# Uncharged preparation work in a one-core encoder layer: k, v blocks and sums of w_out taken out of the convolution's pacing, gate products and last w_out loads moved by a slot or more

## The chip, the core and the metric

The kernel runs on one core of one Trainium2 chip. The core has a matrix engine (TensorE, PE in the profile; the load of its weights is the line PEld) and three others: VectorE (DVE), ScalarE (ACT) and GpSimd (POOL). A fifth engine, SyncE (SP), issues the transfers (DMA). Each engine works off its own instructions in order; between engines, semaphores make an instruction wait for another. The metric is the device time of the one core in microseconds, the median of several runs.

## The reference

One layer of an encoder runs over 18 blocks of 128 tokens (two of a prompt, sixteen of a sample) with 16 learned meta tokens in front. Cut to what matters:

```python
h = rmsnorm(z, norm_w)
proj = einsum('bld,de->ble', h, w_in)                # 1024 -> 2816 columns
q, k, v, g_att, c_val, c_glu, g_conv = split(proj)
q = rmsnorm(q by head, q_norm_w); k = rmsnorm(k by head, k_norm_w)
att = windowed_gqa(q, k, v, sink) * silu(g_att)      # 8 heads, 2 of k and v, window 128, ALiBi, sink
u = c_val * sigmoid(c_glu)                           # 512 channels
y = depthwise convolution of u, width 31, + conv_b
cnv = silu(layernorm(y)) * silu(g_conv)              # norm over the 512 channels
out = z + concat(att, cnv) @ w_out                   # 1024 -> 1024
```

All is float32. A product is made of three passes on PE with operands that are split in a high and a low part.

## The kernel before

**Two chunks, eleven units.** The tokens are cut into six groups of 384 columns (the first 400), three to a chunk. For each chunk PE goes through eleven units of w_in, 256 columns each: four for the convolution's value and gate (U_C), two for the convolution's gate g_conv, two for g_att, one for k and v (U_KV), two for q (U_Q). A projection writes a PSUM tile pj; lines L1014 and L1030 are its matmuls (L1030 has the tokens on the partitions and serves k, v and q, one block of 128 tokens at a time). The last two units, called ws_6 and ws_7 in the program, run in the second chunk beside the layer norm and the first attention blocks.

**The convolution and its pacing.** DVE does the depthwise convolution, 31 taps for each of four channel tiles and each chunk (L1097). The taps wait in a queue in the code, and a small accountant hands them out while the program is written: tick(ns) gives credit for PE time that has passed, every tap takes 1.04 * 1167 + 135 = 1349 from it, and owe(ns) takes credit for other DVE work. So owe has no instruction of its own: it only makes the taps, and what follows them, come later in the program.

**The layer norm.** When a chunk's tap queue has been empty for LN_WAIT ticks (9 in the first chunk, 1 in the second), tick hands out one layer norm block of 128 tokens per call, ten blocks in the second chunk. A block is three steps: four transposes of y into PSUM (lnt, L250) with statistics on DVE (mv) and an inverse root on POOL; the normalisation on DVE into zn (L263, three buffers); four transposes back (lnu, L269), Silu on ACT into the same zn (L272) and a store to cd (L275). The attention later loads it as cn (L445).

**The attention and the output.** After the layer norm come 160 attention slots, eight to a block of 128 queries. A slot holds scores (S, L466), the maximum and exponentials (sb, L524 and L536, with a factor es taken in on POOL, L562), transposes of the probabilities (pT_c, pT_m, pT_x), their copies (ptiles, L588, L598, and on POOL with a mask, L590), the values (O, L616), and a piece of the output product. spread(b), called behind each of the 18 blocks of the two last q units, writes the first 14 slots between them from the eighth block on; attention_rest writes the others. Output products (yb, L721) go by pairs of blocks, 16 slots to a pair, in the order of the table JOBS; the table acts says in which slot of a pair the gate g_conv and the norm are loaded (load_mix: tiles gc and cn), multiplied on POOL (mix_conv, L695), subtracted (mix_diff), split into high and low parts (two_parts, cast on ACT L679, rest on DVE L680), and so on. The first product of a pair is c1, in slot 15.

**w_out.** Instead of four products of 2 by 2 blocks the kernel takes sums and differences of w_out's parts (c1, s1 to s4, t0, t1). presplit_sums makes these 14 operands (seven for each of two halves), in the second chunk beside the convolution, and stores them; pieces come back by load_apart and load_wo. Twelve are loaded from spread (WO_AT); load_wo 12 to 17 and the last load_apart follow in attention_rest. later(k, f) runs f k ticks later; the six loads use the buffers of the projections' operands.

**Who sets the order.** A scheduler places the instructions of each engine by its own estimate of their times. Once the attention's buffers are open, POOL keeps the order of the code instead; in attention_rest PE does too. All transfers go through SP's queue, which holds eight at a time: each waits for the one eight before it.

Of the kernel before, what the change touches and what calls it, by code (L numbers as in the profile page):

```python
# [82 lines left out]
PIECES_W = [("c1", 0), ("c1", 1), ("s3", 0), ("s3", 1), ("s2", 0), ("s2", 1), (6, 0), (6, 1), (7, 0), (7, 1)]  # L83
# [45 lines left out]
def hymba_kernel(  # L129
# [58 lines left out]
    def owe(ns):  # L188
        credit[0] -= ns

    def later(k, f):
        due.setdefault(clock[0] + k, []).append(f)
# [188 lines left out]
    def presplit_sums(i):  # L381

        raw = {}
        for key, e, nh in ((11, 4 + i, 0), (21, i, 0), (12, 4 + i, 1), (22, i, 1)):
            raw[key] = sp.tile([P, 2, 400], F32, tag="xt", name=f"wor{key}_{i}", bufs=XTB)[:, :, :UW]
            src = w_out[e][:, 512 * nh : 512 * nh + 512].rearrange("p (a n) -> p a n", n=UW)
            nc.sync.dma_start(raw[key], src)

        def operand(name, key):
            both = sp.tile([P, D], F32R, tag="xn", name=f"wo{name}_{i}")  # L390
            hi, lo = (both[:, 512 * k : 512 * k + 512].rearrange("p (a n) -> p a n", n=UW) for k in range(2))
            nc.scalar.copy(hi, raw[key])
            nc.vector.tensor_tensor(lo, raw[key], hi, op=ALU.subtract)
            owe(700)
            later(1, lambda: nc.sync.dma_start(wod[PIECES_W.index((name, i))], both.bitcast(F32)))

        def minus(dst, x, y):
            nc.vector.tensor_tensor(raw[dst], raw[x], raw[y], op=ALU.subtract)
            owe(700)

        steps = (
            ("c1", 11, None),
            ("t1", 21, (11, 12, 11)),
            ("s4", 22, (12, 22, 12)),
            ("s1", 11, (22, 22, 11)),
            ("s3", 12, (21, 21, 22)),
            ("s2", 22, None),
            ("t0", 21, None),
        )

        def step(name, key, diff):
            operand(name, key)
            if diff:
                minus(*diff)

        for k, args in enumerate(steps):
            later(2 + k, lambda args=args: step(*args))

    def load_apart(i):
        if i < 2:  # L420
            t = pool["b"].tile([P, D], F32R, tag=f"wa{i}", name=f"wa{i}", bufs=1)
        else:
            t = cst["pt" if i < APART else "rest"][:, 6:8].rearrange("p a n -> p (a n)")
        wo[PIECES_W[i]] = t
        nc.sync.dma_start(t.bitcast(F32), wod[i])

    def load_wo(idx):

        if idx % 3 == 0:
            slot = idx // 3  # L430
            wo_slot[slot] = xp.tile([P, ND, 400], F32R, tag=("xh", "xl")[slot % 2], name=f"wo{slot}")
        flat = wo_slot[idx // 3].rearrange("p a n -> p (a n)")
        i = APART + idx
        t = wo[PIECES_W[i]] = flat[:, D * (idx % 3) : D * (idx % 3) + D]
        nc.sync.dma_start(t.bitcast(F32), wod[i])
# [5 lines left out]
    def load_mix(b):  # L441
        gct[b] = pool["b"].tile([P, 4, P], F32, tag="gc", name=f"gc{b}", bufs=2)
        nc.sync.dma_start(gct[b], gd[4:8, :, P * b : P * b + P].rearrange("j p n -> p j n"))
        cnt[b] = pool["b"].tile([P, 4, P], F32, tag="cn", name=f"cn{b}", bufs=2)
        nc.sync.dma_start(cnt[b].rearrange("p j n -> p (j n)"), cd[b])  # L445
# [236 lines left out]
    def with_rest(f):  # L682
        pending.append(f)
        while "rest" in cst and pending:
            pending.pop(0)()
# [8 lines left out]
    def mix_conv(b):  # L694
        nc.gpsimd.tensor_tensor(cnt[b], cnt[b], gct[b], op=ALU.mult)  # L695

    def mix_diff(p):
        nc.gpsimd.tensor_tensor(temp(0), cnt[2 * p + 1][:, 0:NS, :], cnt[2 * p][:, 0:NS, :], op=ALU.subtract)
        diff[p] = True
# [53 lines left out]
    for p in range(NB // 2):  # L753
        b0, b1 = 2 * p, 2 * p + 1
        for rel, f in (
            (5, lambda b0=b0: load_mix(b0)),
            (7, lambda b1=b1: load_mix(b1)),
            (9, lambda p=p: load_x(p, (0, 1))),
            (10, lambda b0=b0: mix_conv(b0)),
            (11, lambda b1=b1: mix_conv(b1)),  # L760
            (12, lambda p=p: with_rest(lambda: mix_diff(p))),
            (12, lambda p=p: load_x(p, (1, 1))),
            (13, lambda b1=b1: with_rest(lambda: two_parts("c1", cnt[b1][:, 0:NS, :]))),
            (14, lambda: with_rest(lambda: two_parts("s3", temp(0)))),
            (17, lambda b0=b0: two_parts(("c", 0), cnt[b0][:, NS:4, :])),
            (17, lambda p=p: load_x(p, (0, 0))),
            (20, lambda b1=b1: two_parts(("c", 1), cnt[b1][:, NS:4, :])),
            (18, lambda p=p: load_x(p, (1, 0))),
            (18, lambda p=p: add_kept(p, (1, 1), 0)),
            (20, lambda p=p: add_kept(p, (0, 0), 1)),  # L770
            (21, lambda p=p: add_kept(p, (1, 0), 0)),
        ):
            acts.setdefault(16 * p + rel, []).append(f)
        for rel, name, es in JOBS:
            to = late_jobs if name == "s3" else jobs
            if p == LAST and name in ("t1", (1, 0)):
                for c0 in (0, 256):
                    to.setdefault(16 * p + rel, []).append((p, name, es, c0, 256))
            else:
                to.setdefault(16 * p + rel, []).append((p, name, es))  # L780
# [53 lines left out]
    def attention_rest():  # L834
        for _ in range(2):
            tick(0)
        cst["man"].close()
        att_pools.enter_context(tc.manual_schedule(engines=MAN2))
        rest = wl.tile([P, ND, 2, UW], F32R, tag="ws", name="rest")
        cst["rest"] = rest.rearrange("p a b n -> p (a b n)").rearrange("p (i n) -> p i n", n=512)  # L840
        for k in range(6):
            later(1 + k, lambda k=k: load_wo(12 + k))
        later(7, lambda: load_apart(len(PIECES_W) - 1))
        while slots:
            slot_step(*slots.pop(0))
        while work_left():
            tick(3000)
        att_pools.close()
        wr_pools.close()
        left_pools.close()  # L850

    if True:
# [321 lines left out]
        def kv_block(ws, g, o, rows, b):  # L1174
            ps = proj_te(ws, g, o, rows)
            rk = head_norm(ps, rows, KV, f"k{b}")
            vs = sp.tile([P, KV, 2, HD], F32R, tag="vs", name=f"vs{b}", bufs=3)
            pv = ps[:rows, P : 2 * P].rearrange("p (h e) -> p h e", e=HD)
            nc.scalar.copy(vs[:rows, :, 0, :], pv)
            nc.vector.tensor_tensor(vs[:rows, :, 1, :], pv, vs[:rows, :, 0, :], op=ALU.subtract)  # L1180
            vflat = vs[:rows].rearrange("p a b e -> p (a b e)").bitcast(F32)
            store(vmd if b < 0 else vd[b], vflat)
            kn = sp.tile([P, KV, HD], F32, tag="kn", name=f"kn{b}")
            owe(800)

            def fin():
                pk = ps[:rows, 0:P].rearrange("p (h e) -> p h e", e=HD)
                nc.vector.tensor_tensor(
                    kn[:rows],
                    pk,  # L1190
                    rk[:rows, :KV].unsqueeze(2).to_broadcast([rows, KV, HD]),
                    op=ALU.mult,
                )
                later(1, fin2)

            def fin2():
                pt = psum.tile([P, 512], F32, tag="d", name=f"kt{b}")
                nc.tensor.transpose(pt[:, :rows], kn[:rows].rearrange("p a e -> p (a e)"), ident[:rows, :rows])
                ks = sp.tile([P, 2 * P], F32R, tag="ks", name=f"ks{b}")
                nc.scalar.mul(ks[:, :rows], pt[:, :rows], kscale[:, 0:1])  # L1200
                nc.vector.scalar_tensor_tensor(
                    ks[:, rows : 2 * rows], pt[:, :rows], kscale[:, 0:1], ks[:, :rows], op0=ALU.mult, op1=ALU.subtract
                )
                to = (kmd if b < 0 else kd[b]).rearrange("(h p) k l n -> p h k (l n)", h=2)
                for kv in range(KV):
                    part = ks[HD * kv : HD * kv + HD, : 2 * rows].bitcast(F32)
                    store(to[:, :, kv, :], part.unsqueeze(1).to_broadcast([HD, 2, 2 * rows]))

            later(1, fin)
# [262 lines left out]
```

## Time and profile before

| | before |
|---|---|
| time, median of 3 runs | 955.06 us (953.53 to 955.95) |
| profiled execution | 954.25 us, span 952.4 |
| PE busy | 930.4 us, 98% |
| DVE busy | 774.5 us, 81% |
| ACT busy | 449.8 us, 47% |
| POOL busy | 364.1 us, 38% |
| HBM read, written | 115.83 MB, 65.85 MB |

The span goes from the first to the last instruction of the profiled execution; its time is 1.85 us longer. A row of the trace reads: start, duration, engine, line, operation, output <- inputs, shape, count, and in square brackets the idle time before it with what ended it. A row of a stretch reads: from:to, its length, PE's busy time and number of matmuls, the clock that PE was granted (1.00 is full), the mean busy share of the 16 DMA engines, and GB/s. A row of waits reads: who waited, for whom, us in total, times, longest. In the chain of waits each row is a start, a duration and what the end of the program waited for in that time.

### The profile page before, as it was taken

The numbers are of one execution on the slowest core, as the hardware profiler recorded it, in microseconds if no ns is written. First come the engines' busy times: TensorE is split into PE (matmuls) and PEld (weight loads), VectorE is DVE, ScalarE is ACT, GpSimd is POOL, SyncE is SP. The second block draws the span as 40 slices with busy tenths as digits, with TensorE's granted clock in tenths as the row PEclk, the third lists the DMA queues.
The fourth block names the chain that finished last, engine by engine and source line by source line (L and its number), as shares of the span: only waits on it lengthen the run. The fifth ranks groups of instructions, "written<-read, shape, count | busy, mean of one in ns | idle before, by whom it ended". The sixth has DMA issues, their size and how long they took to land.

```text
span 952.4 us, 16892 instructions
## 1 busy us (share of the span) xinstructions
PE 930.4 (98%) x5734; PEld 878.5 (92%) x5734; DVE 774.5 (81%) x1340; ACT 449.8 (47%) x1233; POOL 364.1 (38%) x553
## 2 busy tenths in 40 slices
PE   8999999999999999999999998799999999999998
PEld 8999999999999999999999988677888888888887
DVE  5579999997977779999997545579887887887874
ACT  7432112353458732011112248567676677676762
POOL 4310000273559300000001343587766466555654
PEclk9999999999999999999999999999999999999999
DMA  8584345675755686333334785996556665665421
GB/s 303 168 282 183 133 174 182 249 268 206 226 154 189 204 290 241 133 122 130 138 132 139 212 242 188 380 341 184 173 176 179 177 195 151 182 197 169 133 96 55
DMA packets 146342, 182.80 MB, mean 192 GB/s; under 512 B 40944, under 2 KB 106816, under 8 KB 146128
## 3 DMA queue, kind: packets, MB, share of 16 engines
q1 hardware_dynamic: 146256, 181.72, 58.3%
q8 instruction: 45, 0.74, 0.3%
q14 instruction: 41, 0.34, 0.1%
HBM read 115.83 MB, written 65.85 MB: 191 GB/s over the span
## 4 chain that ended last, share of the span: by engine, by line
PE 81%; DVE 6%; POOL 3%; DMA 3%; ACT 3%; issue 2%; SPq 0%; POOLq 0%; ACTq 0%; DVEq 0%
PE pj L1014 42%; PE yb L721 16%; PE pj L1030 11%; PE O L616 4%; PE S L466 3%; DVE rest L680 1%; PE pT_m L582 1%; PE pT_c L582 1%; DVE ptiles L599 1%; PE pT_x L582 1%; DVE sb L524 1%; DMA cd<-zn 1%; DMA qd<-qr 1%; ACT sb L536 1%; DMA kd<-ks 1%
## 5 line engine op out<-in xcount | busy, mean ns | idle before, releaser
L1014 PE MATMUL pj<-xh,ws 128*128 128x384 f32 (+1 forms) x1536 | 395.9, 338 | 0.1
L1097 DVE SCALAR_TENSOR_TENSOR y<-us,cw,y 128x1167 f32<-128x1167 f32 x240 | 329.2, 1430 | 0.1
L1014 PEld LDWEIGHTS pj<-xh,ws 128*128 128x128 f32 x1536 | 280.0, 188 | 0.4 <-ACT xh L1262 0.4
L1014 PE MATMUL pj<-xl,ws 128*128 128x384 f32 (+1 forms) x768 | 260.9, 340 | 0.1
L721 PE MATMUL yb<-wo,rest 128*128 128x512 f32 (+1 forms) x717 | 190.8, 399 | 0.0
L1030 PE MATMUL pj<-ws,xh 128*128 128x256 f32 (+1 forms) x880 | 165.9, 286 | 3.9 <-ACT sqq L1131 3.7
L721 PEld LDWEIGHTS yb<-wo,rest 128*128 128x128 f32 x717 | 125.9, 189 | 22.6 <-DVE rest L680 0.2
L1014 PEld LDWEIGHTS pj<-xl,ws 128*128 128x128 f32 x768 | 144.1, 188 | 0.5 <-DVE xl L952 0.4
L1030 PEld LDWEIGHTS pj<-ws,xh 128*128 128x128 f32 (+1 forms) x880 | 137.9, 189 | 4.9 <-ACT sqq L1131 3.9
L1030 PE MATMUL pj<-ws,xl 128*128 128x256 f32 (+1 forms) x440 | 125.1, 284 | 0.0
L1122 ACT ACTIVATE go<-pj 128x384 f32<-128x384 f32 x48 | 23.6, 491 | 151.4 <-PE pj L1014 142.8
L536 ACT ACTIVATE sb<-sb,nm 128x304 f32<-128x304 f32 (+5 forms) x144 | 77.9, 541 | 30.6 <-DVE nm L524 28.5
L177 POOL TENSOR_SCALAR ssk<-ssk 128x2 f32<-128x2 f32 x18 | 10.1, 561 | 211.3 <-ACT sqk L1136 209.3
L524 DVE CUSTOM_DVE_ANT_0 sb<-S,bias,vec 128x304 f32<-128x304 f32 (+5 forms) x144 | 73.8, 515 | 20.4 <-PE S L466 19.4
L562 POOL TENSOR_SCALAR sb<-sb,es 128x304 f32<-128x304 f32 (+5 forms) x144 | 78.3, 563 | 24.7 <-PE pT_x L582 9.9
L1030 PEld LDWEIGHTS pj<-ws,xl 128*128 128x128 f32 (+1 forms) x440 | 83.4, 190 | 0.2
L466 PE MATMUL S<-kw,q 128*128 128x304 f32 (+5 forms) x288 | 63.6, 303 | 2.4 <-ACT keptFalse L739 1.2
L466 PEld LDWEIGHTS S<-kw,q 128*128 128x128 f32 x288 | 52.4, 188 | 14.3 <-ACT keptFalse L739 2.3
L177 POOL TENSOR_SCALAR ssq<-ssq 128x4 f32<-128x4 f32 (+2 forms) x55 | 24.9, 453 | 97.7 <-ACT xn L877 72.5
L644 POOL TENSOR_TENSOR at<-at,ga 128x256 f32<-128x256 f32 x36 | 28.0, 777 | 85.7 <-DVE at L638 85.7
L732 DVE TENSOR_TENSOR yo<-yb,yo 128x512 f32<-128x512 f32 (+1 forms) x55 | 36.9, 671 | 14.9 <-PE yb L721 14.8
L990 DVE TENSOR_TENSOR ws<-wraw,ws 128x512 fp32r<-128x512 f32 x50 | 34.8, 726 | 8.2 <-ACT ws L989 8.2
(156 smaller groups left out, 1369.5 us busy)
## 6 DMA issues: line engine op xcount, KB each, us to landing
wd<-ws SPq DMA_DIRECT2D x36, 512.0 KB, 5.9
ws<-wd SPq DMA_DIRECT2D x36, 512.0 KB, 6.3
wraw<-in_w_in SPq DMA_DIRECT2D x52, 256.0 KB, 6.2
xn<-in_z SPq DMA_DIRECT2D x18, 512.0 KB, 5.4
gd<-go SPq DMA_DIRECT2D x48, 192.0 KB, 2.0
wo<-wod SPq DMA_DIRECT2D x18, 512.0 KB, 7.9
yo<-in_z SPq DMA_DIRECT2D x36, 256.0 KB, 3.3
out_y<-yo SPq DMA_DIRECT2D x35, 256.0 KB, 2.4
```

The lines of the kernel that those rows point to most:

```text
L177: nc.gpsimd.tensor_scalar(src, src, scale, eps, op0=ALU.mult, op1=ALU.add)
L466: r = f(*a, **k)
L524: nc.vector.tensor_tensor_reduce(out=sb[:, n, c0:c1], in0=ps[:, 0:w], in1=cst["bias"][:, kv, at + c0 : at + c1], scale=1.0, scalar=nsnk[:, ...
L536: nc.scalar.activation(sb[:, n, c0:c1], sb[:, n, c0:c1], AF.Exp, bias=nm[:, n : n + 1], scale=-1.0, accum_out=rs[:, n : n + 1],)
L562: nc.gpsimd.tensor_scalar(sb[:, k, a0:a1], sb[:, k, a0:a1], es[:, k : k + 1], 1.0, op0=ALU.mult, op1=ALU.mult)
L616: nc.tensor.matmul(opj[b, kv][:, n0:n1], t[:r, kv, :], p[:r, n0:n1], start=(k == "c" and i == 0), stop=(k == "x" and i == len(work) - 1),)
L721: nc.tensor.matmul(ps[:, :n], x[mi][:, i, :], w[wi], start=((name, e) in OPENS and k == 0), stop=(done and e == es[-1] and k == 2), skip_g ...
L732: nc.vector.tensor_tensor(y, ps[:, :n], y, op=ALU.add)
L990: pinned(eng.tensor_tensor(lo, raw[q], hi, op=ALU.subtract), k < 2)
L1014: nc.tensor.matmul(ps[:, :n], ws[:, d, wi, P * half_i : P * half_i + P], x[xi][:, d, o : o + n], start=(k == 0), stop=(k == 3 * ND - 1),)
L1030: nc.tensor.matmul(ps[:rows, :UW], x[xi][:, d, o : o + rows], ws[:, d, wi, :], start=(k == 0), stop=(k == 3 * ND - 1),)
L1097: nc.vector.scalar_tensor_tensor(y[:, yo + o0 : yo + o1], u[:, o0 + k : o1 + k], cw[:, j, k : k + 1], y[:, yo + o0 : yo + o1], op0=ALU.mul ...
```

## The change

The charges of presplit_sums (seven operands and four differences for each half) and of the second chunk's k, v blocks are taken out. The gate and the norm of a pair's second block are loaded one slot earlier (6 instead of 7). For the first pair alone the gate products and their difference move from slots 10, 11 and 12 to 13. The last seven w_out loads come one tick later, the last of them two. Line numbers behind L396 fall by two.

```diff
--- before.py
+++ after.py
@@ -391,12 +391,10 @@
             hi, lo = (both[:, 512 * k : 512 * k + 512].rearrange("p (a n) -> p a n", n=UW) for k in range(2))
             nc.scalar.copy(hi, raw[key])
             nc.vector.tensor_tensor(lo, raw[key], hi, op=ALU.subtract)
-            owe(700)
             later(1, lambda: nc.sync.dma_start(wod[PIECES_W.index((name, i))], both.bitcast(F32)))
 
         def minus(dst, x, y):
             nc.vector.tensor_tensor(raw[dst], raw[x], raw[y], op=ALU.subtract)
-            owe(700)
 
         steps = (
             ("c1", 11, None),
@@ -754,11 +752,11 @@
         b0, b1 = 2 * p, 2 * p + 1
         for rel, f in (
             (5, lambda b0=b0: load_mix(b0)),
-            (7, lambda b1=b1: load_mix(b1)),
+            (6, lambda b1=b1: load_mix(b1)),
             (9, lambda p=p: load_x(p, (0, 1))),
-            (10, lambda b0=b0: mix_conv(b0)),
-            (11, lambda b1=b1: mix_conv(b1)),
-            (12, lambda p=p: with_rest(lambda: mix_diff(p))),
+            (10 + 3 * (p == 0), lambda b0=b0: mix_conv(b0)),
+            (11 + 2 * (p == 0), lambda b1=b1: mix_conv(b1)),
+            (12 + (p == 0), lambda p=p: with_rest(lambda: mix_diff(p))),
             (12, lambda p=p: load_x(p, (1, 1))),
             (13, lambda b1=b1: with_rest(lambda: two_parts("c1", cnt[b1][:, 0:NS, :]))),
             (14, lambda: with_rest(lambda: two_parts("s3", temp(0)))),
@@ -839,8 +837,8 @@
         rest = wl.tile([P, ND, 2, UW], F32R, tag="ws", name="rest")
         cst["rest"] = rest.rearrange("p a b n -> p (a b n)").rearrange("p (i n) -> p i n", n=512)
         for k in range(6):
-            later(1 + k, lambda k=k: load_wo(12 + k))
-        later(7, lambda: load_apart(len(PIECES_W) - 1))
+            later(2 + k, lambda k=k: load_wo(12 + k))
+        later(9, lambda: load_apart(len(PIECES_W) - 1))
         while slots:
             slot_step(*slots.pop(0))
         while work_left():
@@ -1181,7 +1179,7 @@
             vflat = vs[:rows].rearrange("p a b e -> p (a b e)").bitcast(F32)
             store(vmd if b < 0 else vd[b], vflat)
             kn = sp.tile([P, KV, HD], F32, tag="kn", name=f"kn{b}")
-            owe(800)
+            owe(800 if g in CHUNKS[0] else 0)
 
             def fin():
                 pk = ps[:rows, 0:P].rearrange("p (h e) -> p h e", e=HD)
```

The program that is built from it differs in order as follows; the names with numbers are buffers.

First place, PE at the end of the first q unit (ws_6) of the second chunk. lnt and lnu are the layer norm's transposes to and from, zn its normalised blocks, y the convolution's four channel tiles, pj a projection. Before, a block's lnu and another's lnt stand between two q projections:

```order
L1030 MATMUL pj_6113<-ws_6_5128,xh_3484 128x256
L269 MATMUL lnu_5902<-ident,zn_5851 128x128 x4
L250 MATMUL lnt_5945<-ident,y_0_3769 128x128
L250 MATMUL lnt_5945<-ident,y_1_3974 128x128
L250 MATMUL lnt_5945<-ident,y_2_4487 128x128
L250 MATMUL lnt_5945<-ident,y_3_4841 128x128
L1030 MATMUL pj_6201<-ws_7_5540,xh_3036 128x256
```

After:

```order
L250 MATMUL lnt_5817<-ident,y_0_3769 128x128
L250 MATMUL lnt_5817<-ident,y_1_3974 128x128
L250 MATMUL lnt_5817<-ident,y_2_4327 128x128
L250 MATMUL lnt_5817<-ident,y_3_4724 128x128
L269 MATMUL lnu_5772<-ident,zn_5723 128x128 x4
L269 MATMUL lnu_5833<-ident,zn_5783 128x128 x4
L250 MATMUL lnt_5878<-ident,y_0_3769 128x128
L250 MATMUL lnt_5878<-ident,y_1_3974 128x128
L250 MATMUL lnt_5878<-ident,y_2_4327 128x128
L250 MATMUL lnt_5878<-ident,y_3_4724 128x128
L269 MATMUL lnu_5892<-ident,zn_5844 128x128 x4
L1028 MATMUL pj_5940<-ws_6_5140,xh_3262 128x256
```

Ahead of the last rows stand lnu_5642, lnt_5757, the transpose kt_5707 of a k block and lnu_5712 in the same way: the lnu of five blocks now follow each other up to pj_5940 with no projection between.

Second place, ACT between the last q projections (copy qr_17 and square sqq_17 of the last block) and the first cast of the first pair's rest. Before:

```order
L486 CAST q_2_6725<-qT_6720 64x4x4x32
L487 CAST q_2_6725<-qT_6720 64x4x4x32
L1155 COPY qr_15_6555<-pj_6530 128x256
L1131 ACTIVATE sqq_15_6558<-pj_6530 128x256
L1155 COPY qr_16_6604<-pj_6579 128x256
L1131 ACTIVATE sqq_16_6607<-pj_6579 128x256
L588 CAST ptiles<-pT_x_6715 128x128
L636 COPY tmp_0_6727<-O_0_6508 64x512
L1155 COPY qr_17_6651<-pj_6626 128x256
L1131 ACTIVATE sqq_17_6654<-pj_6626 128x256
L679 CAST rest<-cn_6397 128x256
```

After:

```order
L1153 COPY qr_17_6649<-pj_6624 128x256
L1129 ACTIVATE sqq_17_6652<-pj_6624 128x256
L596 CAST ptiles<-pT_c_6659 128x512
L634 COPY tmp_0_6727<-O_0_6508 64x512
L534 ACTIVATE sb_5924,rs_1_6665<-sb_5924,nm_1_6664 128x272
L596 CAST ptiles<-pT_m_6683 128x512
L534 ACTIVATE sb_5924,rs_1_6665<-sb_5924,nm_1_6664 128x240
L586 CAST ptiles<-pT_x_6715 128x128
L534 ACTIVATE sb_5924,rs_1_6665<-sb_5924,nm_1_6664 128x208
L484 CAST q_2_6725<-qT_6720 64x4x4x32
L485 CAST q_2_6725<-qT_6720 64x4x4x32
L677 CAST rest<-cn_6342 128x256
```

The copies and squares of blocks 15 and 16 have moved up, and two casts of probabilities, three exponentials, the copy of the output's part (tmp) and the casts of q_2 now stand between the last projection's square and the cast to rest.

Third place, POOL around the first pair's gate products (cn <- cn, gc). Before:

```order
L523 MEMSET sb_5788 128x32
L695 TENSOR_TENSOR cn_6293<-cn_6293,gc_6291 128x512
L590 TENSOR_TENSOR ptiles<-ptiles,vec 128x512
L523 MEMSET sb_5788 128x64
L695 TENSOR_TENSOR cn_6397<-cn_6397,gc_6395 128x512
L523 MEMSET sb_5788 128x96
L553 TENSOR_TENSOR pm_0_6674<-sb_5788,es_0_6455 128x128
L562 TENSOR_SCALAR sb_5788<-sb_5788,es_0_6455 128x272
L562 TENSOR_SCALAR sb_5788<-sb_5788,es_0_6455 128x240
L562 TENSOR_SCALAR sb_5788<-sb_5788,es_0_6455 128x208
```

After:

```order
L521 MEMSET sb_5932 128x32
L588 TENSOR_TENSOR ptiles<-ptiles,vec 128x512
L521 MEMSET sb_5932 128x64
L521 MEMSET sb_5932 128x96
L551 TENSOR_TENSOR pm_0_6672<-sb_5932,es_0_6455 128x128
L560 TENSOR_SCALAR sb_5932<-sb_5932,es_0_6455 128x272
L560 TENSOR_SCALAR sb_5932<-sb_5932,es_0_6455 128x240
L560 TENSOR_SCALAR sb_5932<-sb_5932,es_0_6455 128x208
L560 TENSOR_SCALAR sb_5932<-sb_5932,es_0_6455 128x176
L693 TENSOR_TENSOR cn_6293<-cn_6293,gc_6291 128x512
L693 TENSOR_TENSOR cn_6342<-cn_6342,gc_6340 128x512
```

The mask (ptiles <- ptiles, vec), pm and the four scalings of sb now stand ahead of the two gate products, which were in front of or between them.

## The prediction

> **What bounds the kernel now.** I read the page first, then PE in stretches of 5 us, then who PE waited for, and last the chain of waits around the stretches that are not full.
>
> ```profile
> span 952.4 us, 16892 instructions
> PE 930.4 (98%) x5734; PEld 878.5 (92%) x5734; DVE 774.5 (81%) x1340; ACT 449.8 (47%) x1233; POOL 364.1 (38%) x553
> PE   8999999999999999999999998799999999999998
> ```
>
> PE is the bound, so a change of order can only win what PE loses: 22.0 us of idle time in all (952.4 - 930.4), and the clock it loses after pauses. Slices 25 and 26 (571 to 619 us) are the only dip in the middle. In stretches (length, PE busy and matmuls, granted clock, DMA share, GB/s):
>
> ```profile
> 550.00:555.00 5.00, 3.96 (x34) 1.00 0.94 237
> ...
> 580.00:585.00 5.00, 3.61 (x32) 1.00 0.46 168
> 585.00:590.00 5.00, 3.99 (x23) 0.66 0.14 53
> ...
> 610.00:615.00 5.00, 2.37 (x11) 1.00 1.06 370
> 615.00:620.00 5.00, 3.15 (x15) 0.66 1.08 336
> ...
> sum 190.00, PE 175.58; mean PE 4.62
> ```
>
> Of the 22 us idle, 14.4 lie between 510 and 700 us (190 - 175.58). This is where the second chunk's k, v and q projections, the layer norm of its convolution and the first two attention blocks stand beside each other. Who PE waited for there (us in total, times, longest):
>
> ```profile
> PE pj L1030 <- ACT sqq L1131: 3.7, 1, 3.7
> PE lnu L269 <- DVE mv L254: 2.4, 1, 2.4
> PE lnu L269 <- DVE zn L263: 2.1, 2, 1.1
> ...
> PE yb L721 <- ACT rest L679: 1.5, 1, 1.5
> PE O L616 <- ACT ptiles L598: 1.2, 1, 1.2
> PE S L466 <- DVE nm L524: 0.6, 1, 0.6
> ```
>
> Two kinds: 4.5 us (2.4 + 2.1) in the layer norm, whose transposes (lnu) wait for normalised blocks; and 7.0 us (3.7 + 1.5 + 1.2 + 0.6) in the first attention blocks, where projections have run out or stand behind something. The chain of waits tells what is behind each:
>
> ```profile
> 555.43 0.97 ACT zn L272 x3
> 556.40 8.91 DMA cd<-zn
> ...
> 607.26 8.85 DMA qd<-qr
> ...
> 616.85 4.29 PE pj L1030 x23
> ```
>
> zn has three buffers, so a block can be normalised only when the store of the block three earlier has landed; that store took 8.91 us. The copy of q to qr, by which PE's next PSUM buffer comes free, waited for a store of 8.85 us. The clock adds to it: after the 2.4 us wait it stood at half speed (stretches of 2 us):
>
> ```profile
> 586.00:588.00 2.00, 1.99 (x10) 0.50 0.00 0
> 588.00:590.00 2.00, 2.00 (x15) 0.74 0.35 132
> ```
>
> That costs 1.0 + 0.5 = 1.5 us; the stretch 615 to 620 shows the same 0.66 for five as 585 to 590, so I count 1.5 there too.
>
> **The charges.** Credit no longer taken: per half of the sums 7 operands and 4 differences at 700, two halves 15,400 ns; 9 blocks of k, v at 800 make 7,200; together 22.6 us, or 16.7 taps at the 1.35 us that the pacing reckons for one. No instruction is removed. The built order says what comes of it: DVE's taps stand where they stood until the last two, so the convolution ends when it did. But the code sees it empty earlier and hands out the layer norm's ten blocks sooner. Their first transposes now stand among the last k, v blocks, and the scores come earlier between the projections of the last q unit. In the order before, eight of that unit's nine blocks were over when the first block's values began, and the three bubbles of 605 to 617 us follow. After, each of the last six projections has attention beside it.
>
> Gone: the layer norm's waits, 4.5 + 1.5 of clock = 6.0; the attention's waits, 7.0 + 1.5 = 8.5. Sum 14.5.
>
> **New wait 1: the layer norm in a bunch.** Five blocks' transposes now follow each other with no projection between (front's first place). Rows for it:
>
> ```profile
> 569.50 0.44 PE lnu L269 x4
> ...
> 574.24 1.51 ACT L272 ACTIVATE zn<-lnu,vec 128x128 f32<-128x128 f32 x4
> ...
> L263 DVE TENSOR_SCALAR zn<-lnt,mv 128x512 f32<-128x512 f32 x10 | 8.1, 809 | 11.4 <-DMA cd<-zn 7.4 <-POOL mv L256 4.0
> ...
> DMA to landing us min/median/max: 2.0/2.5/8.9
> ```
>
> Call the bunch's blocks 1 to 5. Block 4 needs the store of block 1: transpose 0.44, some 0.4 behind a copy on ACT, Silu 1.51, issue 0.1, landing 2.5 (the median of the 18 stores), normalise 0.81: 5.8 us from the bunch's start. PE's own work until then is five transposes of 0.44 and one of k, 2.3: it waits 3.5. Block 5 needs the store of block 2, which stood one Silu behind: some 2.0 more. I take 5.5 and 1.5 of clock, 7.0. The ends: 0, if these stores land under cover (no wait of the first chunk's layer norm is in PE's list), and 13.4, if one of them takes 8.9 instead of 2.5. I take the median since the built store queue now has all of the first six stores ahead of the 1.5 MB table of biases; the store that took 8.91 was issued 3.75 us behind it, at 556.40:
>
> ```profile
> 552.65 0.62 SPq L297 DMA_DIRECT2D bias<-in_bias_c  x1
> ```
>
> [...]
>
> **New wait 2: behind the last projection.** The first product of w_out needs c1's hi part, a cast on ACT. In the built order after, ACT does eleven things between the last projection and this cast (second place). In the order of these rows:
>
> ```profile
> L1131 ACT ACTIVATE sqq<-pj 128x256 f32<-128x256 f32 x18 | 6.5, 387 | 5.1 <-PE pj L1030 4.9 <-DVE ssq L1132 0.2
> L598 ACT CAST ptiles<-pT_c 128x512 fp32r<-128x512 f32 x7 | 4.1, 583 | 3.1 <-PE pT_c L582 3.1
> L636 ACT COPY tmp<-O 64x512 f32<-64x512 f32 x5 | 2.9, 584 | 3.7 <-PE O L616 3.6
> L536 ACT ACTIVATE sb<-sb,nm 128x240 f32<-128x240 f32 x6 | 2.9, 492 | 2.6 <-DVE nm L524 2.6
> L486 ACT CAST q<-qT 64x512 fp32r<-64x512 f32 x5 | 2.9, 575 | 1.0 <-PE qT L466 1.0
> L679 ACT CAST rest<-cn 128x256 fp32r<-128x256 f32 x6 | 2.4, 405 | 0.2 <-PE yb L721 0.2
> ```
>
> And two rows of PE's steady stretch behind the first products:
>
> ```profile
> 637.11 1.63 PE L721 MATMUL yb<-wo,rest 128*128 128x512 f32 x6
> ...
> 639.29 1.63 PE L721 MATMUL yb<-wo,rest 128*128 128x512 f32 x6
> ```
>
> Copy and square 0.39 each, two probability casts and the output's copy 0.58 each, three exponentials 0.49, a small cast (taken as half of 0.58), two q casts 0.58: 5.4; with 0.3 from PE to ACT and the cast itself 0.4, 6.1 us. PE's own work there is an estimate, 3.2: 0.11 a transpose (four in the 0.44 at 569.50), and 0.2 to 0.25 for each matmul of scores or values, since two of each stand with six products and a transpose between the last two rows, 2.18 us apart. So it waits 2.9; with half a chance of losing the clock (0.7) I take 3.6. The ends: 1.5 (the old wait for this cast) and 6.
>
> **The first pair's gate products.** Two multiplications on POOL, before:
>
> ```profile
> 615.83 1.26 POOL L695 TENSOR_TENSOR cn<-cn,gc 128x512 f32<-128x512 f32 x1 [5.43 <-DMA qd<-qr]
> 617.05 1.04 POOL L590 TENSOR_TENSOR ptiles<-ptiles,vec 128x512 fp32r<-128x512 f32 x1
> ```
>
> POOL stood 5.43 us for their data, and the probabilities' mask (L590) behind them. After, mask and softmax scaling go first (third place): part of the 7.0. What is late next: cn and the pair's difference end some 2.5 us (2 x 1.26) behind the scaling. That is about where ACT reaches its cast, so I count nothing; alone it would be 0 to 2.5, which the end of 6 above holds. For pairs after the first only the load of gate and norm is one slot earlier: 0; no wait of PE is for them.
>
> **The last pieces of w_out.** Seven loads, one slot later (the last of them two). The buffers of the first six are those of the last projection's operands, free at 621 us. Before, they were issued and landed thus:
>
> ```profile
> 623.83 2.28 SPq L435 DMA_DIRECT2D wo<-wod  x4
> ...
> wo<-wod SPq DMA_DIRECT2D x18, 512.0 KB, 7.9
> ```
>
> Four issues from 623.83 on and 7.9 to landing end at 634.0 (623.83 + 2.28 + 7.9); the products at 637.11 are the first to read one of them, 3.1 us later. A slot is the 2.18 us between those products and the next, so 0.9 would be left if the issues moved by a whole slot. They need not: in the built store queue these loads keep their neighbours, and the products are put back behind the last projection by new wait 2. I take 0; with a slow landing up to 2. The other move of w_out (its first twelve pieces now stand behind the gates' loads in that queue) helps the row at 607.26: the q stores go among fewer bytes.
>
> **Sum.** -14.5 + 7.0 + 3.6 + 0 + 0 = -3.9 us, on an execution of 954.25 (span 952.4 and 1.85 around it): 950.35. The median of the three runs is 955.06, 0.8 above; on it 951.2. I say 950.8.
>
> **Rivals.** (A) The bunch hardly waits (new wait 1 near 1): -9.9, 945.2. For it: the DMA share was only 0.46 at 580 to 585, and the first chunk's norms made no wait. Against: three buffers, and five blocks in a row. (B) No change: stores of 4 us instead of 2.5 (two on the path, 3.0) and the tail near 5: 0.5 from before, 954.6. For it: with the k stores between them the DMA share was 0.94. (C) Slower: one store on block 4's path takes 8.9 as at 556.40. New wait 1 becomes 13.4 and the sum +2.5, 957.6; two such, 964. It decides from a landing of 6.4 us on. Against: the biases now come behind. [...] That the charges do nothing is excluded by the built order.
>
> **How the numbers follow.** Forecast (948.5 to 953) 0.40, A 0.19, B 0.18, C 0.16, D 0.07. 0.3% (2.9 us) is about what a measurement of this kernel can tell from no change: below 952.2 lie A, D and three quarters of the forecast, 0.56; above 957.9 most of C, by a second slow store or the tail's upper end, 0.14, and a little of B, 0.01; the rest, 0.29, is the same. The range goes from A with the tail at its lower end (2.1 less, 943.1) to C with a little of what is worse, 958.5.
>
> **What would show it.** Right: no ACT table loads between Silu and Exp but one at L534 (five before); PE's dip at 605 to 617 gone; waits of lnu for zn in two or three pieces, 4 to 7 us together near 556 to 566; a wait of yb for rest of 2 to 4 us after the last pj; the first yb at 617 to 620 instead of 623.0. Wrong: store landings of cd far from 2.5, a new wait of PE for a w_out piece, or of POOL for gates.

## The result, and the profile after

The changed kernel takes 951.03 us (median of 13 runs, 948.83 to 953.52) beside 954.61 for the one before on the same chip (13 runs): a ratio of 0.9963, with a 95% interval of 0.9951 to 0.9975. So 0.37% or 3.6 us are won; 950.8 was forecast. Here and below the ratio and its interval are formed from the fast executions alone, so they need not be the quotient of the medians beside them; the 955.08 of the first four experiments counts one slow execution of the kernel before, of 3483.77 us, and without it would be 954.9. The profiled execution took 951.85 us with a span of 950.1. The head of its page:

```profile
span 950.1 us, 16894 instructions
PE 931.0 (98%) x5734; PEld 879.2 (93%) x5734; DVE 774.9 (82%) x1340; ACT 444.6 (47%) x1229; POOL 364.5 (38%) x553
PE   9999999999999999999999979999999999999998
```

PE's idle time fell from 22.0 to 19.1 us (950.1 - 931.0), and its busy time rose by 0.6: it ran at half clock (0.50) for 10.2 us (6.8 from 562.5 on and 3.4 from 620.5 on) instead of 6.8 (3.4 each from 585.6 and 616.3 on). The stretches of 5 us in which PE is not full, or not at full clock (columns as before):

```profile
555.00:560.00 5.00, 3.54 (x30) 1.00 0.59 170
560.00:565.00 5.00, 1.56 (x9) 0.75 0.89 253
565.00:570.00 5.00, 5.00 (x27) 0.57 0.97 313
...
610.00:615.00 5.00, 4.28 (x30) 1.00 1.02 397
615.00:620.00 5.00, 1.58 (x7) 1.00 1.03 397
620.00:625.00 5.00, 5.00 (x20) 0.66 1.03 412
```

The waits of 554, 566, 584 to 586 and 605 to 617 us are gone, as is the half clock behind them; a hole at 557 to 565 and one at 616 to 619 have come, each with half clock behind it. The second is the wait of 1.5 us that the first product had at 623 before, now longer. PE's rows that end an idle time there (in brackets how long, and who was waited for):

```profile
558.03 0.66 PE L269 MATMUL lnu<-ident,zn 128*128 128x128 f32 x4 [1.05 <-ACT zn L272]
561.85 0.63 PE L269 MATMUL lnu<-ident,zn 128*128 128x128 f32 x4 [2.26 <-DVE zn L263]
564.82 1.09 PE L269 MATMUL lnu<-ident,zn 128*128 128x128 f32 x4 [1.59 <-DVE mv L254]
...
619.36 2.33 PE L719 MATMUL yb<-wa,rest 128*128 128x512 f32 x6 [3.11 <-ACT rest L677]
```

These are the two new waits of the forecast, at its two places: 4.9 us in the layer norm's bunch (1.05 + 2.26 + 1.59) and 3.1 us ahead of the first product. That product begins at 619.36 instead of 623.02. Who held its cast back is told by ACT's and POOL's own rows:

```profile
616.87 0.58 ACT L485 CAST q<-qT 64x512 fp32r<-64x512 f32 x1
618.90 0.40 ACT L677 CAST rest<-cn 128x256 fp32r<-128x256 f32 x1 [1.45 <-POOL cn L693]
...
616.38 2.48 POOL L693 TENSOR_TENSOR cn<-cn,gc 128x512 f32<-128x512 f32 x2
```

ACT was through its eleven things at 617.45 and then stood 1.45 us for the second gate product, which the change had put behind the softmax scaling. So the wait is where it was forecast, but the forecast's reason, the length of ACT's queue, gives only a part of it: with the gate products in time the cast would in this order have begun at 617.45 and the first product at 617.9, and some 1.7 of the 3.1 us would have stayed.

### The profile page after: what moved, and what is told of

It is laid out like the page before. It is cut to its first block, busy times and chain, and to the rows that moved or that the text cites. A ratio compares the mean times of both kernels' runs of the same rounds, so it can differ in the third digit from the quotient of the medians.

```text
span 950.1 us, 16894 instructions
## 1 busy us (share of the span) xinstructions
PE 931.0 (98%) x5734; PEld 879.2 (93%) x5734; DVE 774.9 (82%) x1340; ACT 444.6 (47%) x1229; POOL 364.5 (38%) x553
## 4 chain that ended last, share of the span: by engine, by line
PE 86%; DVE 6%; POOL 3%; ACT 2%; issue 1%; DMA 1%; SPq 0%; DVEq 0%; ACTq 0%; POOLq 0%
PE pj L1012 42%; PE yb L719 16%; PE pj L1028 15%; PE O L614 4%; PE S L464 3%; PE pT_c L580 1%; PE pT_m L580 1%; DVE rest L678 1%; DVE ptiles L597 1%; PE pT_x L580 1%; DVE sb L522 1%; ACT sb L534 1%; DMA vm<-vd 1%; PE lnu L269 1%; PE lnt L250 1%
## 5 line engine op out<-in xcount | busy, mean ns | idle before, releaser
L719 PEld LDWEIGHTS yb<-wo,rest 128*128 128x128 f32 x717 | 125.9, 189 | 22.6 <-DVE rest L678 0.2
L534 ACT ACTIVATE sb<-sb,nm 128x304 f32<-128x304 f32 (+5 forms) x144 | 77.9, 541 | 31.8 <-DVE nm L522 29.7
L560 POOL TENSOR_SCALAR sb<-sb,es 128x304 f32<-128x304 f32 (+5 forms) x144 | 76.3, 547 | 24.7 <-DVE es L547 10.7
```

The lines of the kernel that those rows point to most:

```text
L534: nc.scalar.activation(sb[:, n, c0:c1], sb[:, n, c0:c1], AF.Exp, bias=nm[:, n : n + 1], scale=-1.0, accum_out=rs[:, n : n + 1],)
L560: nc.gpsimd.tensor_scalar(sb[:, k, a0:a1], sb[:, k, a0:a1], es[:, k : k + 1], 1.0, op0=ALU.mult, op1=ALU.mult)
L719: nc.tensor.matmul(ps[:, :n], x[mi][:, i, :], w[wi], start=((name, e) in OPENS and k == 0), stop=(done and e == es[-1] and k == 2), skip_g ...
```

## The experiments

Before the runs, the built order says that three parts of the change do nothing by themselves. With w_out's last pieces put back to their old ticks, or with the load of gate and norm put back to slot 7, every engine's rows stand as after the whole change. With the k, v charge alone taken out, or with the sums charged 350 instead of 700, they stand as before. The reason for the last is in the code: at the start of the first q unit all taps left are handed out anyway (`while conv_q[0] or conv_q[1]: tick(3000)`), so credit matters only where it empties the queue earlier than that, inside the k, v unit. What is left to tell apart is: the sums' charge, the k, v charge once the sums' is gone, and the first pair's gate products.

**The charges alone** (whole change without the moves of gate products, loads and w_out pieces):

```diff
-            owe(700)        # two places in presplit_sums
-            owe(800)
+            owe(800 if g in CHUNKS[0] else 0)
```

> The charges of the sums and of the second chunk's k, v blocks taken out, nothing else: gate products, their loads and w_out's last pieces stand where they stood. Theory 1 (the charges carry the gain, and the moved gate products are what the first product of w_out now waits for): the layer norm's three waits stay as after the whole change (4.9 us together), but the gate products are done early, in a gap of POOL, and the 3.1 us wait of yb for rest falls below 1 us; with the clock 2 to 4 us less than after the whole change, so 946.5 to 949.5 beside a before of 954.6 (ratio 0.9915 to 0.9945). Rival 1 (the moved gate products are part of the gain): POOL stands again for the gates' loads ahead of the mask, 2 us or more, and the time is the same as after the whole change or worse, 951 to 954 (ratio 0.9963 to 0.9995).

Measured: 946.68 us beside 955.08, ratio 0.9923 (0.9908 to 0.9937), twice the gain of the whole change. The layer norm's waits stay; the first product waits no more. PE's, POOL's and ACT's rows:

```profile
562.01 0.63 PE L269 MATMUL lnu<-ident,zn 128*128 128x128 f32 x4 [1.63 <-DVE zn L263]
565.03 1.09 PE L269 MATMUL lnu<-ident,zn 128*128 128x128 f32 x4 [1.95 <-DVE mv L254]
...
615.71 1.63 PE L719 MATMUL yb<-wa,rest 128*128 128x512 f32 x6
...
609.26 1.29 POOL L693 TENSOR_TENSOR cn<-cn,gc 128x512 f32<-128x512 f32 x1
611.78 1.27 POOL L693 TENSOR_TENSOR cn<-cn,gc 128x512 f32<-128x512 f32 x1
...
612.97 0.59 ACT L596 CAST ptiles<-pT_m 128x512 fp32r<-128x512 f32 x1
613.45 0.41 ACT L677 CAST rest<-cn 128x256 fp32r<-128x256 f32 x1
```

The gate products run at 609.26 and 611.78 without any wait for their loads, and the first product begins at 615.71, 3.65 us earlier than after the whole change. Theory 1 holds, rival 1 falls. But the move of the gate products had changed two things, and this run takes back both. POOL is in time again, and ACT's cast stands at 613.45 behind two casts of probabilities only; the exponentials, the output's copy and the casts of q come behind it. So that the cast stood behind eleven things came from the moved products too, and not from the charges.

**The gate products alone** (with the loads and pieces; here the earlier load passes one store of q in SP's queue and is issued at 611.57 instead of 612.54):

```diff
-            (10, lambda b0=b0: mix_conv(b0)),
-            (11, lambda b1=b1: mix_conv(b1)),
-            (12, lambda p=p: with_rest(lambda: mix_diff(p))),
+            (10 + 3 * (p == 0), lambda b0=b0: mix_conv(b0)),
+            (11 + 2 * (p == 0), lambda b1=b1: mix_conv(b1)),
+            (12 + (p == 0), lambda p=p: with_rest(lambda: mix_diff(p))),
```

> The charges stay as before; only the first pair's gate products, the load of gate and norm and w_out's last pieces are moved. Theory 1: nothing, ratio 0.999 to 1.001, since the waits of 605 to 617 us are for q projections and stores; a wait of yb for rest may grow by up to 1 us. Rival 1: the mask no longer stands behind products that wait for their data, and 1 to 3.7 us are won (ratio 0.996 to 0.999).

Measured: 952.71 beside 955.08, ratio 0.9977 (0.9966 to 0.9988). Alone they win a little, so rival 1 holds here and theory 1 does not. POOL's rows, and PE's wait for the q projections:

```profile
611.34 1.04 POOL L590 TENSOR_TENSOR ptiles<-ptiles,vec 128x512 fp32r<-128x512 f32 x1
...
615.74 1.26 POOL L695 TENSOR_TENSOR cn<-cn,gc 128x512 f32<-128x512 f32 x1 [0.23 <-DMA cn<-cd]
618.36 1.28 POOL L695 TENSOR_TENSOR cn<-cn,gc 128x512 f32<-128x512 f32 x1 [1.35 <-DMA cn<-cd]
...
616.74 0.58 PE L1030 MATMUL pj<-ws,xh 128*128 128x256 f32 x1 [2.46 <-ACT sqq L1131]
```

The mask L590 runs at 611.34 instead of 617.05, and PE waits 2.46 us instead of 3.67 for the projection's buffer, though at 597.28 a new wait of 0.52 stands. The products still wait for their loads, at 615.74 and 618.36. That is the difference: without the uncharged layer norm the loads of cn land at about 616 and 618, and it is right to let the mask pass; with it they are issued some 18 and 22 us earlier. How much of the 0.23% is the mask and how much the clock stays open, for in the profiled execution only one of the two half-clock stretches of before is left (616.3 to 619.7 us). SP's rows, before and after the whole change:

```profile
605.92 0.33 SPq L445 DMA_DIRECT2D cn<-cd  x1
612.54 1.57 SPq L445 DMA_DIRECT2D cn<-cd  x1
```

```profile
588.20 0.53 SPq L443 DMA_DIRECT2D cn<-cd  x1
590.39 1.46 SPq L443 DMA_DIRECT2D cn<-cd  x1
```

**The sums' charge alone:**

```diff
-            owe(700)        # two places in presplit_sums
```

> Only the charges of the sums taken out (15.4 of 22.6 us of credit); the k, v charges stay. In the built program the k, v charge alone taken out gives the very order of before on every engine, so it can only matter together with the sums. Theory 1 (the gain comes with the place of the layer norm, in proportion): most of the gain of the charges alone, 947 to 951 (ratio 0.992 to 0.996). Rival 2 (a threshold: the layer norm must begin inside the k, v blocks to pay): less than a third of it, 952.5 to 955 (ratio 0.998 to 1.0005).

Measured: 943.19 beside 955.08, ratio 0.9883 (0.9866 to 0.990), better than either theory had it, and the fastest kernel of this study. So the k, v charge is not a lesser part of the same gain: taking it out as well costs 3.5 us. PE's head and waits:

```profile
span 941.3 us, 16895 instructions
PE 926.8 (98%) x5734; PEld 875.3 (93%) x5734; DVE 775.3 (82%) x1340; ACT 444.7 (47%) x1229; POOL 368.2 (39%) x553
...
557.76 0.63 PE L269 MATMUL lnu<-ident,zn 128*128 128x128 f32 x4 [1.23 <-DVE zn L263]
559.10 0.63 PE L269 MATMUL lnu<-ident,zn 128*128 128x128 f32 x4 [0.27 <-DVE zn L263]
...
612.19 2.03 PE L719 MATMUL yb<-wa,rest 128*128 128x512 f32 x6 [1.04 <-ACT rest L677]
```

The layer norm waits 1.5 us instead of 4.6 with all charges gone, and no half clock is left in the span (mean clock 1.0). The first product waits 1.0 us, which it did not with all charges gone. The two profiled spans are 5.1 us apart (946.4 and 941.3). In their first 50 us, ahead of anything that the edit moves, PE was busy for 46.91 us here and for 48.46 there. Behind them it is idle 2.5 us less here and busy 2.6 less. The busy time is clock: with all charges gone PE worked 5.17 us at half clock (0.50) between 563.6 and 570.2, behind the bunch, where three matmuls of a projection took 0.64 us instead of 0.35, so that by estimate 2.3 us of it are lost. The first product comes 3.5 us earlier (612.19 and 615.71); what is won behind it no run here takes apart.

**Four zn buffers** in the changed kernel:

```diff
-            st["zn"] = yp.tile([P, 512], F32, tag="zn", name=f"zn{b}", bufs=3)
+            st["zn"] = yp.tile([P, 512], F32, tag="zn", name=f"zn{b}", bufs=4)
```

> The whole change, with four buffers instead of three for the normalised blocks (zn). Theory 1 (the bunch waits for the stores of three blocks earlier): the waits of lnu fall from 4.9 to below 2.5 us and some of the lost clock comes back; 2.3 to 4.5 us less than the whole change, 946.5 to 948.8 beside a before of 954.6 (ratio 0.9915 to 0.994). Rival 3 (the waits are the length of the chain transposes, statistics, inverse root, normalisation, and a free buffer changes nothing): 4 to 5 us of lnu waits stay, time as after the whole change, 950 to 952 (ratio 0.995 to 0.9975).

Measured: 950.09 beside 955.08, ratio 0.9956 (0.9942 to 0.9969): as after the whole change. PE's waits in the bunch:

```profile
560.81 0.63 PE L269 MATMUL lnu<-ident,zn 128*128 128x128 f32 x4 [1.16 <-DVE mv L254]
563.68 0.63 PE L269 MATMUL lnu<-ident,zn 128*128 128x128 f32 x4 [1.81 <-DVE zn L263]
```

With the 1.05 at 558.08 they make 4.0 us instead of 4.9. After the whole change one normalisation of the bunch waited for a store:

```profile
560.89 0.81 DVE L263 TENSOR_SCALAR zn<-lnt,mv 128x512 f32<-128x512 f32 x1 [0.79 <-DMA cd<-zn]
```

With four buffers none of them does. Rival 3 holds: the store is one link, and where it is taken away the block's own chain of transposes, statistics, inverse root and normalisation is nearly as long. The next run puts work of PE between the blocks instead.

**Blocks spread.** All charges gone, a block at most at every second call in the second chunk:

```diff
-        if ln_q and not flushing[0] and ln_q[0][0]():
+        if ln_q and not flushing[0] and clock[0] >= ln_at[0] + 2 * ln_c[0] and ln_q[0][0]():
...
+                ln_c[0] = c     # ahead of the loop that makes the blocks
```

> All charges taken out, as in the run of the charges alone, and in the second chunk a layer norm block is handed out at most at every second call instead of every call. Theory 5 (the k, v charge pays because without it the transposes of five blocks follow each other with no projection between): with the blocks spread the lnu waits fall from 4.6 us to below 2 and no half clock stays between 540 and 575 us; 941.5 to 945 (ratio 0.986 to 0.990). Rival 5 (uncharged k, v blocks cost by something else, or the spread blocks only move the waits into the attention behind them): 946 us or more (ratio 0.9905 and up).

Measured: 947.47 beside 954.30, ratio 0.9923 (0.9905 to 0.994), the same as the charges alone. PE in two stretches, of this kernel and then of the charges alone:

```profile
540.00:575.00 35.00, 35.00 (x302) 1.00 0.86 276
605.00:625.00 20.00, 16.10 (x76) 0.83 1.03 346
```

```profile
540.00:575.00 35.00, 30.22 (x236) 0.90 0.77 249
605.00:625.00 20.00, 18.39 (x122) 1.00 1.04 391
```

The mechanism of theory 5 is shown: with the blocks apart PE does not wait once between 540 and 575 us. But its time was missed and rival 5's second half holds: the attention now begins later, and a projection again waits 2.1 us at 609 and the first product 1.3, with half clock behind both (0.50 from 610 to 613 and from 617 to 619). So the bunch is why PE waits in the layer norm; that the kept k, v charge wins its 3.5 us by this alone is not shown.

**The gate products on top of the sums** (the whole change with the k, v charge kept):

```diff
-            owe(800 if g in CHUNKS[0] else 0)
+            owe(800)
```

> The whole change, but the second chunk's k, v blocks are charged as before (so: the sums uncharged, and the gate products, loads and last pieces of w_out moved). Theory 4 (behind the softmax scaling the two gate products of 1.26 us each stand on the way to c1's cast, whatever the rest of the order): the wait of yb for rest grows from the 1.0 us of the sums alone to 2 to 4 us, 944.5 to 947.5 beside a before of 955 (ratio 0.989 to 0.9925). Rival 4 (the move helps, as it did alone by 0.23%, and only hurts without a projection behind the scaling): here a projection does stand there, so the same as the sums alone or better, 941.5 to 943.5 (ratio 0.986 to 0.9885).

Measured: 944.80 beside 954.30, ratio 0.9895 (0.9875 to 0.9914), at the near edge of theory 4 in time, though not in its wait; beside the sums alone the intervals overlap, so the time is unclear. The rows are not:

```profile
610.90 2.52 POOL L693 TENSOR_TENSOR cn<-cn,gc 128x512 f32<-128x512 f32 x2
...
613.45 0.40 ACT L677 CAST rest<-cn 128x256 fp32r<-128x256 f32 x1 [0.41 <-POOL cn L693]
```

ACT waits for POOL again, but with a projection behind the scaling only 0.41 us, and the first product waits 1.57 instead of 1.04 (2 to 4 were expected). So the moved products cost what of them does not fit between the scaling and the cast: 0.5 us of wait here. After the whole change 1.45 us of ACT's time went to them.

**The second pair's product behind the mask,** on top of the sums:

```diff
-            (10, lambda b0=b0: mix_conv(b0)),
+            (10 + (p == 1), lambda b0=b0: mix_conv(b0)),
```

> The sums uncharged, and the second pair's first gate product (not the first pair's) one slot later, behind the mask of the probabilities instead of ahead of it; nothing else in the order of PE and POOL changes. Theory 6 (POOL's queue is in order, so the 1.67 us for which the values wait for the mask at 644 us are the 1.29 us of the product ahead of it and what stands by): that wait falls to below 0.6 us and the time by 1.0 to 1.5 us against the sums alone, 941.6 to 942.3 (ratio 0.987 to 0.988). Rival 6: the mask waits for its own data, the wait stays and the time is 943.0 to 943.5.

Measured: 943.82 beside 954.30, ratio 0.9884 (0.9864 to 0.9903): as the sums alone. The wait for the mask fell from 1.67 to 0.24 us, as theory 6 said. PE's row of the sums alone, then POOL's and PE's rows of this kernel:

```profile
643.82 0.51 PE L614 MATMUL O<-ptiles,vm 128*128 128x512 f32 x1 [1.67 <-POOL ptiles L588]
...
642.69 1.04 POOL L588 TENSOR_TENSOR ptiles<-ptiles,vec 128x512 fp32r<-128x512 f32 x1
643.69 2.74 POOL L693 TENSOR_TENSOR cn<-cn,gc 128x512 f32<-128x512 f32 x2
...
643.79 0.50 PE L614 MATMUL O<-ptiles,vm 128*128 128x512 f32 x1 [0.24 <-POOL ptiles L588]
```

Its time was not won: at 654 the values wait 0.47 for the next mask, and between 540 and 600 us, where PE's and POOL's orders are those of the sums alone, PE idled 1.7 us more in this execution. A single wait of this size is below what these runs can tell.

**Four zn buffers on top of the sums** (the buffer edit above):

> The sums uncharged, with four zn buffers. With all charges gone a fourth buffer took the lnu waits only from 4.9 to 4.1 us. Here the waits for zn are 1.5 us. If they are waits for stores they go, 1 to 1.5 us less than the sums alone (941.6 to 942.3); if they are the chain of a block, nothing changes (942.8 to 943.6).

Measured: 945.48 beside 954.30, ratio 0.9896 (0.9877 to 0.9914), outside both expectations. The buffer makes the scheduler place the blocks otherwise, and a projection then waits:

```profile
607.23 0.58 PE L1028 MATMUL pj<-ws,xh 128*128 128x256 f32 x1 [2.94 <-ACT sqq L1129]
```

So this run says nothing on the store; it shows how easily the order behind the layer norm loses 3 us.

## Why the prediction was right, and where it was not

- **Gone, 14.5 us.** Right, but for one wait: the 1.5 us of the first product for its cast are not gone, they have become new wait 2. After the whole change 1.0 us of small waits (0.40 and 0.62 of the values for their probabilities) stand there as well.
- **The charges as one term.** Failed. It took 22.6 us of credit as one quantity that shifts the layer norm. The runs showed a threshold (the k, v charge alone, and half the sums' charge, give the order of before) and then no proportion: 15.4 us of credit bring 1.17%, all 22.6 bring 0.77%. The k, v part, which the forecast counted among the gains, costs 3.5 us.
- **New wait 1, 5.5 and 1.5 of clock.** The place and the size held: 4.9 us, and 6.8 us at half clock, in which PE was busy for some 5 (1.81 and 3.40), so by estimate about 2.5 of clock. The reason was half right. The store of block 1 landed in 2.33 us (2.5 assumed) and ends one of the three waits; the others are a block's own length, and a fourth buffer took only 0.9 us off the sum.
- **New wait 2, 2.9 and 0.7 of clock.** Measured 3.1 and 3.4 us at half clock; that the wait came out so near is luck. From the end of the last projection (611.2) to the end of the cast ACT took 8.1 us instead of 6.1: 1.45 were the wait for POOL, for which the forecast said "I count nothing", and 0.87 a wait of an exponential for DVE. PE had 5.0 us to fill it instead of 3.2: 4.0 of work and the small waits of 1.0. The two errors nearly cancel. And the wait stood under the wrong edit: with the charges alone the cast stands behind two things, not eleven, and PE does not wait.
- **The first pair's gate products, 0.** Failed, in a way that the loads' rows could have told. The row names a store of q as what ended POOL's 5.43 us, but the load of cn was issued at 605.92 and took 9.8 us, until 615.7: POOL stood for its load, and the same change moved this load 18 us forward. The edit answers a lateness that the other edit removes. Alone each wins (0.23% and 0.77%); together they win 0.37%. And "no wait of PE is for them", said of the later pairs, overlooked the second pair: PE's 1.7 us for the mask behind its gate product fell to 0.24 when the product was moved.
- **The last pieces of w_out, and the earlier load, 0.** Right, for a simpler reason than the cover that was worked out: the built order does not move.
- **Sum, -3.9.** The medians differ by 3.6, the profiled spans by 2.3. The right size rests in part on the two errors of new wait 2 that cancel.
- **The signs.** The first product came at 619.4 (617 to 620 foretold); the waits of lnu made 4.9 us in three pieces at 557 to 565 (4 to 7 near 556 to 566); the wait of yb for rest was 3.1 (2 to 4). Where ACT loaded its tables five times between 577 and 595 us (1.28 us each), for the exponential and Silu in turn, it loads one, at L534 (579.86).
- **Rivals.** A and C needed a store under cover or a late one on the path; the one on the path took 2.33 us. Late stores came behind it: those issued at 564.09 and 567.77, behind the table of biases, took 9.5 and 8.6 us, and PE stood for neither, since projections followed. B's terms add up to +0.5, not -0.5, so 955.6; neither its stores nor its tail of 5 came. The 0.07 of D has no run behind it: the clock stood at 0.50 with the 2.40 us wait at 586 before, behind the bunch's waits of 1.05, 2.26 and 1.59, and behind the 3.11 of the first product. "That the charges do nothing is excluded by the built order" was true of the whole, and not of the k, v part; an order of each part would have shown it without any time.

## What to carry to other kernels

Two edits that each cure the same lateness do not add up: ask of each what it answers, and whether the other has taken that away already; here the gate products' move was a gain of 0.23% where their loads came late and cost about 0.4% where they came early. Where a pacing rule with a forced emptying behind it sets the order, its charges act by threshold and by luck of the order, so build each part's order by itself before costing it. And a kernel whose bound engine is 98% busy is won on the few places where that engine has nothing else between two links of a chain: more work between the links (the kept k, v charge) did what a further buffer did not.

## What the runs showed of the hardware

In the profiles PE's half clock (0.50) lasted 3.4 us (before, from 585.6 and 616.3 on; after the whole change from 620.5 on) or 6.8 us (after the whole change from 562.5 on, with the charges alone from 563.5 on). It did not begin at one place beside the wait: after the whole change the clock fell 1.1 us after the 3.1 us wait had ended, before it fell 0.4 us ahead of the end of the 2.40 us wait at 586.0. Stretches ahead of, in and behind the slow one after the whole change:

```profile
617.00:620.40 3.40, 1.04 (x4) 1.00 1.03 412
620.60:623.80 3.20, 3.20 (x13) 0.50 1.03 413
624.00:625.00 1.00, 1.00 (x6) 1.00 1.00 393
```

With the gate products alone, a wait of 2.23 us at 584 to 586.5 cost no clock at all, while before a wait of 2.40 us at the same place did. In the stretch of 582.2 to 585.6 before PE was busy for 1.41 of 3.40 us, there for 2.07; rows of the one and the other:

```profile
582.20:585.60 3.40, 1.41 (x12) 1.00 0.32 116
585.80:589.00 3.20, 2.99 (x14) 0.50 0.12 45
```

```profile
582.20:585.60 3.40, 2.07 (x19) 1.00 0.37 133
585.60:589.00 3.40, 2.49 (x22) 1.00 0.00 0
```

Behind the 2.26 us wait after the whole change the clock fell too, at 562.5. PE's busy share just ahead does not tell when it falls: with four zn buffers in the whole change it fell at 612.7 behind a stretch in which PE was busy for 2.44 of 3.40 us, and it stood at 1.00 from 560 to 570, though PE was busy for only 1.06 us from 560 to 563. It also fell with no single long wait: with the gate products on top of the sums, behind lnu waits of 1.23 and 0.50 us:

```profile
556.50:559.90 3.40, 1.67 (x14) 1.00 1.07 297
560.00:563.20 3.20, 3.20 (x17) 0.50 1.00 338
```

What decides when it falls, these runs do not show.

Most of the scatter between executions of one kernel goes with the granted clock. The changed kernel's spans go in steps: 947.0 and 947.8 at a mean granted clock of 0.998, 948.6 to 950.1 at 0.995 to 0.996, 951.2 to 951.7 at 0.993. The sums alone ran four times at 1.0 within 943.05 to 943.75. So the waits of 2 to 3 us on the bound engine cost their length and, in executions with half clock behind them, an estimated 1.5 to 1.7 us more for each 3.4 us of it in which PE had work (0.64 us against 0.35 for three matmuls with the charges alone make 1.5, the clock of 0.50 makes 1.7). That shorter waits cost no clock is not so: the sums with the gate products, with no wait above 1.7 us, ran two of four times at 0.998. But the three kernels without a longer wait were the steadiest: their four or five runs lie within 0.6 to 0.8 us, those of the others within 1.9 to 5.0.
